# The MLP's operands taken in another order: second half of the tokens projected first, quadrant B21 finished and used last

## The chip, the cores and the metric

The kernel runs on one core of one Trainium2 chip. The metric is the time of one execution on the device, in microseconds (us). The engines of the core work side by side, each through its own list of instructions in order: TensorE (PE) multiplies matrices, VectorE (DVE), ScalarE (ACT) and GpSimd (POOL) work on elements, SyncE (SP) issues most transfers. They meet at semaphores: an instruction waits until the values that it needs have been made, and until the places that it writes have been read by all who still need them.

## The reference, cut to what matters

One layer on 1024 tokens of width 1024: a mixer (forgetting attention beside gated linear attention), a cross-attention on 256 memory tokens, and an MLP of hidden width 4096. Each sub-layer works on the RMS norm of h and adds to h.

```python
h = h + parallel_mixer(rms_norm(h, norm_mix_g), w_in, ..., w_out)
h = h + memory_cross_attention(rms_norm(h, norm_xattn_g), rms_norm(mem, norm_mem_g), ...)   # ends with o @ wo
u = jax.nn.relu(rms_norm(h, norm_mlp_g) @ mlp_w1)
h = h + (u * u) @ mlp_w2
```

All of it is fp32.

## The kernel before, in words

**Products.** fp32 precision is kept with three matmuls for each product: each operand is split into an upper part (a rounded copy, made by ACT) and a lower part (what is left, made by DVE). `gemm` issues, for each 128 rows of the contraction, upper x upper (L107), upper x lower (L108) and lower x upper (L109). `split_into` (L1034) makes a split: ACT's copy is at L1038, DVE's subtraction at L1039. `evac_split` does the same on 512 columns (L114, L115).

**State.** `h`, the transposed activations, lies in SBUF as 8 blocks k of 128 features by 1024 tokens; a *half* is 512 tokens. The MLP is multiplied by the Strassen-Winograd scheme: features and tokens are cut in two, which gives the quadrants b11, b12, b21, b22 of the activations, and seven products replace eight. Its operands are b11, b21, b22 and the combinations t1 = b12 - b11, t2 = b22 - t1, t3 = b22 - b12, t4 = b21 - t2. Each stands in a tile `x` with both parts, 128 x 2048 elements each.

**Order around the change.** `xattn` (the cross-attention) stores its output o through HBM (`od`). `project_o_first` and `project_o_rest` load it (tiles oh, ol; `load_o`) and multiply by wo, in blocks of 24 matmuls (`o_block`), one for each k and half; each adds into h (L841). `finish` (L879 to L883) adds the block's squares to the norm's sum (ACT L165, POOL L166), stores h for the end (`hd`) and scales h in place (DVE L883). Half 0 of the tokens comes before half 1. b11 and b21 are split when half 0 is done; t2 is made block by block beside the last four blocks of half 1 (L909 to L914); t1, t3, b22 and t4 are split at the start of `mlp`.

**The seven stages.** `products7` runs the seven products as stages in the order of `STAGES`. A stage does, for each of two weight blocks (two q), 12 matmuls into a PSUM bank named x, y or w. Every bank is read after each stage (`hidden` in the first product, W1; `output` in the second, W2), also where the next stage adds to the same bank; so that next stage may not start before the bank has been read. In `hidden` the first read of a bank is a copy by ACT (L1131), the later ones are additions by DVE (L1139). They are put into h itself, whose contents are by then split: with `h4`, position c of `c[:, c]` is k 0 (for the first q; 2 for the second) half 0, k 0 half 1, k 1 half 0, k 1 half 1. W1 takes eight rounds p of two q; the results u go to HBM (`ud`), and W2 loads them as its operands into the tiles of the first product's operands, in chunks of 4, 3, 3, 3, 3 q. `weights7` loads a weight block and makes its seven combinations (a11, a12, s1 to s4, a22), each split.

The program is written in this order, but a list scheduler, which knows the cost of each instruction, sets the final order on each engine. The norm's factor of the last step is taken from the squares of the whole h (`token_squares`, `spread`) during W1 and only used at the end.

Of the kernel before, what the change touches and what calls it, by code (L numbers as in the profile page):

```python
# [17 lines left out]
F32 = mybir.dt.float32  # L18
# [12 lines left out]
P = 128  # L31
# [20 lines left out]
class Layer:  # L52
# [774 lines left out]
    def load_o(self, op, half):  # L827

        oh = self.T(op, [P, KT, 512], F32R, "oh")
        ol = self.T(op, [P, KT, 512], F32R, "ol")  # L830
        for k in (slice(k, k + 2) for k in range(0, KT, 2)):
            self.nc.sync.dma_start(f(oh[:, k, :]), self.od[:, 0, half, k, :])
            self.nc.sync.dma_start(f(ol[:, k, :]), self.od[:, 1, half, k, :])
        self.O.append(([oh[:, k, :] for k in range(KT)], [ol[:, k, :] for k in range(KT)]))

    def o_block(self, W, n, half, i, ps, out=None):

# [4 lines left out]

    def project_o_first(self):

        self.ost, self.O = ExitStack(), []
        self.load_o(self.open(self.ost, "op0", side="right"), 0)
        self.Wo = self.wsplit(self.wo[:, 0:512], None)
        for i in range(4):
            self.o_block(self.Wo, 0, 0, i, self.T(self.mmp, [P, 512], F32, "mm"))

    def project_o_rest(self, mx):


        nc = self.nc
        kw = dict(reuse_waits="tile")
        with ExitStack() as st:
            xp = self.open(st, "xp")
# [12 lines left out]
            self.load_o(op1, 1)  # L870
            for i in range(4):
                self.o_block(W, 1, 0, i, next(banks))
            self.ost.close()
            self.acc = [self.T(p, [P, 512], F32, "acc") for p in (xp, self.open(mx, "acc", side="right"))]
            self.X, self.XB = {}, {}
            x0 = self.open(mx, "x0", 3, side="right", **kw)
            h = lambda k, half: self.h[:, k, half * 512:(half + 1) * 512]

            def finish(k, half, src, first):  # L879

                self.add_squares(xp, src, half, first)
                nc.sync.dma_start(self.hd[:, k, half * 512:(half + 1) * 512], src)
                nc.vector.scalar_tensor_tensor(h(k, half), src, self.cols[:, C_MLP + k:C_MLP + k + 1], sB[:, half, :], ALU.mult, ALU.mult)  # L883

            for k in range(KT):
                finish(k, 0, h(k, 0), k == 0)
                if k % 4 == 3:
                    self.operand(("b11", "b21")[k // 4], x0, self.h[:, k - 3:k + 1, 0:512])
            self.token_squares(0, self.yv[:, 0:4])
            for i in range(4):  # L890
                t = self.T(xp, [P, 512], F32, "h2", bufs=2)
                self.o_block(W, 1, 1, i, next(banks), t)
                finish(4 + i, 1, t, i == 0)
            wst.close()
            self.raw7 = self.open(mx, "raw7", 2, side="right", **kw)
            self.ga = self.open(mx, "g7a", 2, side="right", **kw)
# [5 lines left out]
            X = self.X["t2"] = self.T(x0, [P, 2, 4, 512], F32R, "x7")  # L902
            for i in range(4):
                t = self.T(xp, [P, 512], F32, "h2", bufs=2)
                self.o_block(self.Wo, 0, 1, i, next(banks), t)
                finish(i, 1, t, False)
                t2 = self.T(self.s7, [P, 2, 512], F32, "s7")[:, 0, :]
                b11, b21, b12, b22 = h(i, 0), h(4 + i, 0), h(i, 1), h(4 + i, 1)
                nc.vector.tensor_tensor(b11, b12, b11, ALU.subtract)  # L909
                nc.vector.tensor_tensor(t2, b22, b11, ALU.subtract)  # L910
                nc.scalar.activation(X[:, 0, i], t2, AF.Copy)
                nc.vector.tensor_tensor(X[:, 1, i], t2, f(X[:, 0, i]), ALU.subtract)
                nc.vector.tensor_tensor(b12, b22, b12, ALU.subtract)
                nc.vector.tensor_tensor(b21, b21, t2, ALU.subtract)  # L914
            self.XB["t2"] = [X[:, 0, i] for i in range(4)], [X[:, 1, i] for i in range(4)]

    def operand(self, key, pool, src):

# [4 lines left out]
    def xattn(self):  # L923
        nc = self.nc
        with ExitStack() as st:
# [80 lines left out]
            units = [(n, u) for n in range(2) for u in range(4)]  # L1006
            q = []
            for i, (n, u) in enumerate(units):
                if u == 0:
# [18 lines left out]

    STAGES = (("x", "a11", "b11"), ("w", "a12", "b21"), ("x", "s2", "t2"), ("y", "s1", "t1"), ("x", "s3", "t3"),
              ("y", "s4", "b22"), ("x", "a22", "t4"))

    def split_into(self, t, src, n):  # L1034

# [6 lines left out]
    def weights7(self, srcs, n, eng):  # L1042
# [14 lines left out]
        for src, o in zip(srcs, out):  # L1057
            raw = self.T(self.raw7, [P, 4, 512], F32, "raw7")[:, :, 0:n]
            nc.sync.dma_start(raw, src)
            g(o, ("a11", "a12"), raw[:, 0:2])  # L1060
            raws.append(raw)
        yield
        for raw, o in zip(raws, out):
            s = self.T(self.s7, [P, 2, 512], F32, "s7")[:, :, 0:n]
            eng.tensor_tensor(s[:, 0], raw[:, 3], raw[:, 2], ALU.add)  # L1065
            eng.tensor_tensor(s[:, 1], s[:, 0], raw[:, 0], ALU.subtract)
            g(o, ("s1", "s2"), s)
            sa.append(s)
        for raw, o, s2 in zip(raws, out, sa):
            s = self.T(self.s7, [P, 2, 512], F32, "s7")[:, :, 0:n]  # L1070
            eng.tensor_tensor(s[:, 0], raw[:, 0], raw[:, 3], ALU.subtract)
# [1 line left out]
            sb.append(s)  # L1073
        for raw, o, s in zip(raws, out, sb):
            g(o, ("s3", "s4"), s)
            g(o, ("a22",), raw[:, 2:3])
        yield out

    def products7(self, A, B, nk, taken):
# [12 lines left out]
    def mlp(self, mx):  # L1092
        nc = self.nc
        kw = dict(reuse_waits="tile")
        h, X, B = self.h, self.X, self.XB
        x1 = self.open(mx, "x1", 4, **kw)
        self.g4p = self.open(mx, "g74", 2, **kw)
        gb = self.open(mx, "g7b", 2, **kw)
        self.gps, self.ng = [self.ga, self.ga, gb, gb], 2
        my = self.open(mx, "my6", 4, space=PSUM, **kw)  # L1100
# [12 lines left out]
            return next(w)  # L1113

        A = next(self.W1)
        for key, k, half in (("t1", 0, 0), ("t3", 0, 1), ("b22", 4, 1), ("t4", 4, 0)):
            self.operand(key, x1, h[:, k:k + 4, half * 512:(half + 1) * 512])

# [3 lines left out]
        for p in range(NQ // 2):  # L1122
# [3 lines left out]
            def hidden(i, j, ps):  # L1126

                c, t, q = h4[:, i], h4[:, 2 + i], 2 * p + i
                v = c[:, (0, 0, 1, 2, 2, 1, 3)[j]]
                if j in (0, 2, 3):  # L1130
                    nc.scalar.activation(v, ps, AF.Copy)  # L1131
                elif j == 6:
                    nc.scalar.activation(v, ps, AF.Relu)
# [36 lines left out]
        for nk in CHUNKS:  # L1170
# [18 lines left out]
            for o in (0, 2):  # L1189
# [5 lines left out]
                                  nk * P, nc.gpsimd)  # L1195

                def output(i, j, ps):
                    k, half = ((0, 0), (0, 0), (0, 1), (1, 1), (1, 1), (0, 1), (1, 0))[j]
                    k, ts = 2 * (o + i) + k, slice(half * 512, (half + 1) * 512)
                    y = h[:, k, ts]  # L1200
                    if first and j in (0, 2, 3, 6):
# [3 lines left out]
                    if last and j in (1, 4, 5, 6):  # L1205
# [12 lines left out]
def _layout(inputs):  # L1218
# [21 lines left out]
    cols[32:40, C_FB] = a["fox_b_f"]  # L1240
    d["cols"] = cols

    order = [0, 1, 3, 2]
    d["mlp_w1"] = a["mlp_w1"].reshape(2, 4, P, NQ, 2, P).transpose(3, 2, 4, 0, 1, 5).reshape(NQ, P, 4, 512)[:, :, order]
# [21 lines left out]
```

## Time and profile before

| | us |
|---|---|
| three timed runs, median | 1484.55 |
| their lowest and highest | 1483.95, 1484.77 |
| the profiled execution | 1480.27 |
| its span in the profile | 1478.6 |
| PE busy in it | 1430.0 (97%), 7058 matmuls |
| DVE, ACT, POOL busy | 920.8, 681.2, 430.8 |
| mean granted clock of TensorE | 0.988 |

The profile describes one execution. A row of a timeline gives start, duration, engine, line, operation, output tile and inputs, and in brackets how long the engine stood idle before it and what ended that. In a row of windows stand, for a stretch of time, the busy time of each engine with its number of instructions, TensorE's granted clock, the busy share of the DMA engines, and GB/s. A row of waits gives who waited for whom: us in total, how often, and the longest.

The projection of the cross-attention's output lies between about 740 and 847 us of the span, W1 from 847 to about 1177, W2 behind it.

### The profile page before, as it was taken

How to read it: one execution, taken by the hardware profiler on the slowest of the kernel's cores; microseconds unless marked ns; L12 is line 12 of the kernel's file. 1: busy time of each engine (PE TensorE's matmuls, PEld its weight loads, DVE VectorE, ACT ScalarE, POOL GpSimd, SP SyncE). 2: the span in 40 equal slices, each digit the busy share in tenths (PEclk: the TensorE clock that was granted, in tenths of full speed). 3: DMA queues.
4: the chain of work that ended last, by engine and by line, in shares of the span. 5: the costliest groups of instructions: out<-in, count | busy, mean ns of one | idle time of the engine just before them, and what ended most of it. 6: DMA issues, size and time to landing. Idle time of an engine off the chain costs nothing.

```text
span 1478.6 us, 19173 instructions
## 1 busy us (share of the span) xinstructions
PE 1430.0 (97%) x7058; PEld 1195.3 (81%) x7058; DVE 920.8 (62%) x1322; ACT 681.2 (46%) x1092; POOL 430.8 (29%) x457
## 2 busy tenths in 40 slices
PE   7999999999998998999999979999999999999998
PEld 6777788887887787888888868888888888888886
DVE  4396422427776676656654875765565848788686
ACT  4473332326776555445442344544444736335230
POOL 3157503323463412522212300000000342433454
PEclk9999999999999999999999989999999999999999
DMA  8424530259677752413285113544444846337353
GB/s 273 122 54 121 143 86 1 72 173 261 187 203 193 192 158 74 155 40 104 72 279 219 52 63 146 210 171 171 170 169 149 291 159 229 129 109 233 113 201 114
DMA packets 125118, 223.94 MB, mean 151 GB/s; under 512 B 8384, under 2 KB 66528, under 8 KB 118368
## 3 DMA queue, kind: packets, MB, share of 16 engines
q1 hardware_dynamic: 125024, 222.71, 47.0%
q8 instruction: 56, 0.92, 0.2%
q14 instruction: 38, 0.31, 0.1%
HBM read 150.59 MB, written 72.09 MB: 151 GB/s over the span
## 4 chain that ended last, share of the span: by engine, by line
PE 78%; DMA 8%; DVE 7%; ACT 3%; issue 1%; POOL 1%; SPq 0%; POOLq 0%; ACTq 0%; DVEq 0%
PE mm L107 13%; PE mm L108 12%; PE mm L109 12%; PE my L109 7%; PE my L107 7%; PE my L108 7%; PE tr L107 3%; PE tr L108 3%; PE tr L109 3%; DMA raw<-in_w_in_dram 2%; DMA raw<-in_xattn_wkv_dram 2%; PE tr L661 1%; PE pv L668 1%; PE pv L669 1%; PE s L621 1%
## 5 line engine op out<-in xcount | busy, mean ns | idle before, releaser
L109 PE MATMUL my<-x,g 128*128 128x512 f32 x472 | 184.7, 392 | 5.9 <-DVE g L1039 5.8
L107 PE MATMUL my<-x,g 128*128 128x512 f32 x472 | 185.0, 392 | 2.8 <-ACT g L1038 2.8
L108 PE MATMUL my<-x,g 128*128 128x512 f32 x472 | 184.6, 391 | 0.0
L1065 POOL TENSOR_TENSOR s<-raw 128x384 f32<-128x384 f32 (+1 forms) x20 | 25.9, 1297 | 372.0 <-DMA raw<-in_mlp_w_dram 341.4
L1038 ACT ACTIVATE g<-s 128x1024 fp32r<-128x1024 f32 (+1 forms) x72 | 69.0, 963 | 132.8 <-PE my L109 62.3
L108 PE MATMUL mm<-wl,xh 128*128 128x512 f32 x320 | 126.5, 396 | 3.6 <-DVE wl L97 3.6
L107 PE MATMUL mm<-wh,xh 128*128 128x512 f32 x320 | 127.4, 400 | 1.4 <-DVE sq L298 1.4
L109 PE MATMUL mm<-wh,xl 128*128 128x512 f32 x320 | 126.3, 395 | 0.0
L109 PEld LDWEIGHTS my<-x,g 128*128 128x128 f32 x472 | 89.1, 189 | 25.5 <-DVE g L1039 7.0
L107 PEld LDWEIGHTS my<-x,g 128*128 128x128 f32 x472 | 89.2, 189 | 21.8 <-ACT g L1038 3.0
L108 PEld LDWEIGHTS my<-x,g 128*128 128x128 f32 x472 | 89.2, 189 | 18.5
L1039 DVE TENSOR_TENSOR g<-s,g 128x1024 fp32r<-128x1024 f32 (+1 forms) x72 | 85.0, 1186 | 11.1 <-ACT g L1038 10.7
L107 PE MATMUL mm<-x,g 128*128 128x512 f32 x228 | 89.3, 392 | 0.0
L108 PE MATMUL mm<-x,g 128*128 128x512 f32 x228 | 89.2, 391 | 0.0
L109 PE MATMUL mm<-x,g 128*128 128x512 f32 x228 | 88.8, 390 | 0.0
L632 POOL TENSOR_SCALAR p<-p,rrec 128x128 f32<-128x128 f32 (+3 forms) x64 | 50.8, 796 | 128.0 <-DVE rrec L631 115.4
L1039 DVE TENSOR_TENSOR g<-raw,g 128x1024 fp32r<-128x1024 f32 (+3 forms) x72 | 65.4, 910 | 34.2 <-ACT g L1038 34.2
L1178 DVE TENSOR_TENSOR x<-x 128x1024 fp32r<-128x1024 f32 (+1 forms) x64 | 74.4, 1184 | 11.4 <-ACT x L1177 11.1
L97 DVE SCALAR_TENSOR_TENSOR wl<-raw,cols,wh 128x512 fp32r<-128x512 f32 x64 | 49.8, 816 | 48.0 <-ACT wh L96 42.8
L1038 ACT ACTIVATE g<-raw 128x1024 fp32r<-128x1024 f32 (+3 forms) x72 | 55.2, 769 | 48.2 <-PE my L109 20.6
L107 PE MATMUL mm<-wh,sh 128*128 128x512 f32 x192 | 76.3, 399 | 0.7 <-DVE mkv L118 0.4
L108 PE MATMUL tr<-x,g 128*128 128x512 f32 x196 | 76.2, 389 | 0.0
(309 smaller groups left out, 3786.5 us busy)
## 6 DMA issues: line engine op xcount, KB each, us to landing
ud<-h SPq DMA_DIRECT2D x32, 1024.0 KB
x<-ud SPq DMA_DIRECT2D x48, 512.0 KB
raw<-in_mlp_w_dram SPq DMA_DIRECT2D x20, 1024.0 KB
raw<-in_mlp_w_dram SPq DMA_DIRECT2D x16, 768.0 KB
raw<-in_w_in_dram SPq DMA_DIRECT2D x23, 512.0 KB
raw<-in_xattn_wkv_dram SPq DMA_DIRECT2D x16, 512.0 KB
od<-o SPq DMA_DIRECT2D x32, 256.0 KB
xt<-in_x_dram SPq DMA_DIRECT2D x8, 512.0 KB
```

The source lines that it names most:

```text
L97: nc.vector.scalar_tensor_tensor(wl, r, g, f(wh), ALU.mult, ALU.subtract)
L107: mm(ps, lh[k], rh[k], start=start and k == 0, stop=False, **kw)
L108: mm(ps, lh[k], rl[k], start=False, stop=False, **kw)
L109: mm(ps, ll[k], rh[k], start=False, stop=stop and k == n - 1, **kw)
L621: nc.tensor.matmul(ps[:, c], qa[:, ts], ka[:, c], start=True, stop=False)
L632: nc.gpsimd.tensor_scalar(p[:, 0:n], p[:, 0:n], rr, 1.0, ALU.mult, ALU.mult)
L661: nc.tensor.transpose(o, pp[i][:, kb * P:(kb + 1) * P], self.ident)
L668: nc.tensor.matmul(pv, va[:, kb, :], th[:, js], start=kb == 0, stop=False)
L1038: self.nc.scalar.activation(hi, src, AF.Copy)
L1039: self.nc.vector.tensor_tensor(lo, src, f(hi), ALU.subtract)
L1065: eng.tensor_tensor(s[:, 0], raw[:, 3], raw[:, 2], ALU.add)
L1178: nc.vector.tensor_tensor(lo, f(lo), f(hi), ALU.subtract)
```

## The change

The cross-attention's second set of heads takes its token units in the order 2, 3, 0, 1, and the projection does half 1 of the tokens before half 0. The two feature halves are renamed (the rows of W1 are exchanged in the host's layout), so that b11 and b12 are the features of k 4 to 7, and b22 and b21 those of k 0 to 3. b21 is then h of k 0 to 3, half 0, the last four blocks to be projected. b11 and t2 are split during the four blocks before these. The stages are put in the order b11, t1, t2, b22, t3, b21, t4, with the banks x, y, x, y, x, w, x in turns; which reads are copies by ACT changes accordingly. In `mlp`, t1, b22, t3 and b21 are split first; then t2 is put together again from its two parts (L1119), t4 = b21 - t2 is made in place of b21 (L1120) and split. W1's first weight block is loaded and prepared earlier and in another order (a11 first, a12 and a22 last). The squares of half 0 are summed up after p = 1, and the spread comes after p = 3; both came after p = 0.

```diff
     def project_o_first(self):
-        self.load_o(self.open(self.ost, "op0", side="right"), 0)
+        self.load_o(self.open(self.ost, "op0", side="right"), 1)
...
-                self.o_block(self.Wo, 0, 0, i, self.T(self.mmp, [P, 512], F32, "mm"))
+                self.o_block(self.Wo, 0, 1, i, self.T(self.mmp, [P, 512], F32, "mm"))
...
             for k in range(KT):
-                finish(k, 0, h(k, 0), k == 0)
-                if k % 4 == 3:
-                    self.operand(("b11", "b21")[k // 4], x0, self.h[:, k - 3:k + 1, 0:512])
-            self.token_squares(0, self.yv[:, 0:4])
+                finish(k, 1, h(k, 1), k == 0)
+            self.token_squares(1, self.yv[:, 4:8])
...
+                self.o_block(W, 1, 0, i, next(banks), t)
+                finish(4 + i, 0, t, i == 0)
+                t2 = self.T(xp, [P, 512], F32, "t2", bufs=2)
+                b11, b12, b22 = h(4 + i, 0), h(4 + i, 1), h(i, 1)
+                self.evac_split(X1[:, 0, i], X1[:, 1, i], b11)
+                nc.vector.tensor_tensor(b11, b12, b11, ALU.subtract)
+                nc.vector.tensor_tensor(t2, b22, b11, ALU.subtract)
+                self.evac_split(X2[:, 0, i], X2[:, 1, i], t2)
+                nc.vector.tensor_tensor(b12, b22, b12, ALU.subtract)
...
-    STAGES = (("x", "a11", "b11"), ("w", "a12", "b21"), ("x", "s2", "t2"), ("y", "s1", "t1"), ("x", "s3", "t3"),
-              ("y", "s4", "b22"), ("x", "a22", "t4"))
+    STAGES = (("x", "a11", "b11"), ("y", "s1", "t1"), ("x", "s2", "t2"), ("y", "s4", "b22"), ("x", "s3", "t3"),
+              ("w", "a12", "b21"), ("x", "a22", "t4"))
...
-        for key, k, half in (("t1", 0, 0), ("t3", 0, 1), ("b22", 4, 1), ("t4", 4, 0)):
-            self.operand(key, x1, h[:, k:k + 4, half * 512:(half + 1) * 512])
+        half = lambda k, i: h[:, k:k + 4, i * 512:(i + 1) * 512]
+        for key, src in (("t1", half(4, 0)), ("b22", half(0, 1)), ("t3", half(4, 1)), ("b21", half(0, 0))):
+            self.operand(key, x1, src)
+        t2, t4 = half(4, 0), half(0, 0)
+        nc.vector.tensor_tensor(t2, f(X["t2"][:, 0]), f(X["t2"][:, 1]), ALU.add)
+        nc.vector.tensor_tensor(t4, t4, t2, ALU.subtract)
+        self.operand("t4", x1, t4)
...
-                v = c[:, (0, 0, 1, 2, 2, 1, 3)[j]]
-                if j in (0, 2, 3):
+                v = c[:, (0, 2, 1, 1, 2, 0, 3)[j]]
+                if j in (0, 1, 2):
                     nc.scalar.activation(v, ps, AF.Copy)
...
-            if p == 0:
-
-                self.token_squares(1, self.yv[:, 4:8])
+            if p == 1:
+
+                self.token_squares(0, self.yv[:, 0:4])
...
+            if p == 3:
                 F = self.T(self.s7, [P, 2, 512], F32, "s7")
```

The order of ACT at the start of `mlp`, before. The tiles x_1903 to x_1906 are t1, t3, b22 and t4; my_8579 and my_8593 are the banks of stage 0, s and g weights:

```order
619 L1038 ACTIVATE x_1903_8567<-h_5812 128x2048
620 L911 ACTIVATE x_1876_8363<-s_1892_8513 128x512
621 L1038 ACTIVATE x_1904_8570<-h_5812 128x2048
622 L1038 ACTIVATE x_1905_8573<-h_5812 128x2048
623 L1038 ACTIVATE x_1906_8576<-h_5812 128x2048
624 L1131 ACTIVATE h_5812<-my_8579 128x512
625 L1131 ACTIVATE h_5812<-my_8593 128x512
626 L1038 ACTIVATE g_1894_8540<-s_1893_8537 128x1024
```

The same place with the change. x_1902 to x_1906 are t1, b22, t3, b21 and t4; my_8583 and my_8597 are the banks of stages 0 and 2, my_8611 and my_8625 those of stage 1:

```order
621 L1037 ACTIVATE g_1898_8554<-s_1896_8548 128x1024
622 L1037 ACTIVATE g_1899_8557<-s_1897_8551 128x1024
623 L165 ACTIVATE sqT_8529<-h_1893_8502 128x512
624 L1037 ACTIVATE x_1902_8566<-h_5812 128x2048
625 L1037 ACTIVATE x_1903_8569<-h_5812 128x2048
626 L1037 ACTIVATE x_1904_8572<-h_5812 128x2048
627 L1037 ACTIVATE x_1905_8575<-h_5812 128x2048
628 L1037 ACTIVATE x_1906_8580<-h_5812 128x2048
629 L1135 ACTIVATE h_5812<-my_8583 128x512
630 L1135 ACTIVATE h_5812<-my_8597 128x512
631 L1135 ACTIVATE h_5812<-my_8611 128x512
632 L1135 ACTIVATE h_5812<-my_8625 128x512
```

In both orders the first banks are copied behind the copy of t4. With the change that copy of t4 has a new row of DVE before it (L1120), and the banks' copies write into the part of h that t4 is split from. DVE's order there, from the last block of the projection on (mm_8503 is its bank):

```order
775 L841 TENSOR_TENSOR h_1893_8502<-mm_8503,h_5812 128x512
776 L883 SCALAR_TENSOR_TENSOR h_5812<-h_1893_8502,cols_72,sB_7964 128x512
777 L1038 TENSOR_TENSOR g_1898_8554<-s_1896_8548,g_1898_8554 128x1024
778 L1038 TENSOR_TENSOR g_1899_8557<-s_1897_8551,g_1899_8557 128x1024
779 L1038 TENSOR_TENSOR x_1902_8566<-h_5812,x_1902_8566 128x2048
780 L1038 TENSOR_TENSOR x_1903_8569<-h_5812,x_1903_8569 128x2048
781 L1119 TENSOR_TENSOR h_5812<-x_1860_8212 128x4x512
782 L1038 TENSOR_TENSOR x_1904_8572<-h_5812,x_1904_8572 128x2048
783 L1038 TENSOR_TENSOR x_1905_8575<-h_5812,x_1905_8575 128x2048
784 L1120 TENSOR_TENSOR h_5812<-h_5812 128x4x512
785 L1038 TENSOR_TENSOR x_1906_8580<-h_5812,x_1906_8580 128x2048
```

Rows 775 to 784 all stand before t4's split in row 785. The third place is ACT's order at the change from W1 to W2, with the change. mm_10345 is the last bank of W1, x_1905 the tile of b21, into which W2's operands are loaded, L1182 ACT's copy of such an operand:

```order
803 L1138 ACTIVATE h_5812<-h_5812 128x512
804 L1182 ACTIVATE x_1904_8572<-x_1904_8572 128x1024
805 L1037 ACTIVATE g_2076_10611<-s_2074_10605 128x1024
806 L1137 ACTIVATE h_5812<-mm_10345 128x512
807 L1182 ACTIVATE x_1905_8575<-x_1905_8575 128x1024
808 L1146 ACTIVATE h_5812<-h_5812 128x1536
809 L1037 ACTIVATE g_2073_10602<-s_2072_10599 128x1024
810 L1182 ACTIVATE x_1905_8575<-x_1905_8575 128x1024
```

Row 807 waits for a load into a tile that stage 5 of W1's last round still reads; g_2073 is a weight of W2's first round.

More of the change, by code (lines that the diff above doesn't have):

```diff
@@ L833, in load_o @@
             self.nc.sync.dma_start(f(ol[:, k, :]), self.od[:, 1, half, k, :])
-        self.O.append(([oh[:, k, :] for k in range(KT)], [ol[:, k, :] for k in range(KT)]))
+        self.O[half] = [oh[:, k, :] for k in range(KT)], [ol[:, k, :] for k in range(KT)]
     def o_block(self, W, n, half, i, ps, out=None):
@@ L843, in project_o_first @@
     def project_o_first(self):
-        self.ost, self.O = ExitStack(), []
-        self.load_o(self.open(self.ost, "op0", side="right"), 0)
+        self.ost, self.O = ExitStack(), {}
+        self.load_o(self.open(self.ost, "op0", side="right"), 1)
         self.Wo = self.wsplit(self.wo[:, 0:512], None)
         for i in range(4):
-            self.o_block(self.Wo, 0, 0, i, self.T(self.mmp, [P, 512], F32, "mm"))
+            self.o_block(self.Wo, 0, 1, i, self.T(self.mmp, [P, 512], F32, "mm"))
     def project_o_rest(self, mx):
@@ L869, in project_o_rest @@
             self.wps = wps
-            self.load_o(op1, 1)
+            self.load_o(op1, 0)
             for i in range(4):
-                self.o_block(W, 1, 0, i, next(banks))
+                self.o_block(W, 1, 1, i, next(banks))
             self.ost.close()
-            self.acc = [self.T(p, [P, 512], F32, "acc") for p in (xp, self.open(mx, "acc", side="right"))]
-            self.X, self.XB = {}, {}
-            x0 = self.open(mx, "x0", 3, side="right", **kw)
+            self.acc = [self.T(p, [P, 512], F32, "acc") for p in (self.open(mx, "acc", side="right"), xp)]
+            x0 = self.open(mx, "x0", 2, side="right", **kw)
             h = lambda k, half: self.h[:, k, half * 512:(half + 1) * 512]
@@ L885, in project_o_rest @@
             for k in range(KT):
-                finish(k, 0, h(k, 0), k == 0)
-                if k % 4 == 3:
-                    self.operand(("b11", "b21")[k // 4], x0, self.h[:, k - 3:k + 1, 0:512])
-            self.token_squares(0, self.yv[:, 0:4])
+                finish(k, 1, h(k, 1), k == 0)
+            self.token_squares(1, self.yv[:, 4:8])
+            X1, X2 = (self.T(x0, [P, 2, 4, 512], F32R, "x7") for _ in range(2))
+            self.X = {"b11": X1, "t2": X2}
+            self.XB = {n: tuple([X[:, j, i] for i in range(4)] for j in range(2)) for n, X in self.X.items()}
             for i in range(4):
                 t = self.T(xp, [P, 512], F32, "h2", bufs=2)
-                self.o_block(W, 1, 1, i, next(banks), t)
-                finish(4 + i, 1, t, i == 0)
+                self.o_block(W, 1, 0, i, next(banks), t)
[7 more added lines that the diff above has]
+                nc.vector.tensor_tensor(b12, b22, b12, ALU.subtract)
             wst.close()
             self.raw7 = self.open(mx, "raw7", 2, side="right", **kw)
+            self.g4p = self.open(mx, "g74", 2, side="right", **kw)
             self.ga = self.open(mx, "g7a", 2, side="right", **kw)
@@ L900, in project_o_rest @@
             next(self.W1)
-            X = self.X["t2"] = self.T(x0, [P, 2, 4, 512], F32R, "x7")
             for i in range(4):
                 t = self.T(xp, [P, 512], F32, "h2", bufs=2)
[L905 to L915, printed above, removed]
+                self.o_block(self.Wo, 0, 0, i, next(banks), t)
+                finish(i, 0, t, False)
     def operand(self, key, pool, src):
@@ L1004, in attend @@
                                                   u % 2 * 256:u % 2 * 256 + 256], f(o[:, i]))
-            units = [(n, u) for n in range(2) for u in range(4)]
+            units = [(0, u) for u in range(4)] + [(1, u) for u in (2, 3, 0, 1)]
             q = []
             for i, (n, u) in enumerate(units):
-                if u == 0:
+                if i % 4 == 0:
                     weights(n)
@@ L1059, in weights7 @@
             nc.sync.dma_start(raw, src)
-            g(o, ("a11", "a12"), raw[:, 0:2])
+            g(o, ("a11",), raw[:, 0:1])
             raws.append(raw)
-        yield
         for raw, o in zip(raws, out):
@@ L1068, in weights7 @@
             sa.append(s)
+        yield
         for raw, o, s2 in zip(raws, out, sa):
@@ L1075, in weights7 @@
             g(o, ("s3", "s4"), s)
-            g(o, ("a22",), raw[:, 2:3])
+        for raw, o in zip(raws, out):
+            g(o, ("a12", "a22"), raw[:, 1:3])
         yield out
@@ L1095, in mlp @@
         h, X, B = self.h, self.X, self.XB
-        x1 = self.open(mx, "x1", 4, **kw)
-        self.g4p = self.open(mx, "g74", 2, **kw)
+        x1 = self.open(mx, "x1", 5, **kw)
         gb = self.open(mx, "g7b", 2, **kw)
@@ L1197, in output @@
                 def output(i, j, ps):
-                    k, half = ((0, 0), (0, 0), (0, 1), (1, 1), (1, 1), (0, 1), (1, 0))[j]
+                    k, half = ((0, 0), (1, 1), (0, 1), (0, 1), (1, 1), (0, 0), (1, 0))[j]
                     k, ts = 2 * (o + i) + k, slice(half * 512, (half + 1) * 512)
                     y = h[:, k, ts]
-                    if first and j in (0, 2, 3, 6):
+                    if first and j in (0, 1, 2, 6):
                         nc.scalar.activation(y, ps, AF.Copy)
@@ L1204, in output @@
                         nc.vector.tensor_tensor(y, ps, y, ALU.add)
-                    if last and j in (1, 4, 5, 6):
+                    if last and j in (3, 4, 5, 6):
                         nc.vector.tensor_tensor(y, y, F[:, half], ALU.mult)
@@ L1241, in _layout @@
     d["cols"] = cols
-    order = [0, 1, 3, 2]
-    d["mlp_w1"] = a["mlp_w1"].reshape(2, 4, P, NQ, 2, P).transpose(3, 2, 4, 0, 1, 5).reshape(NQ, P, 4, 512)[:, :, order]
+    order, swapped = [0, 1, 3, 2], [1, 0, 2, 3]
+    d["mlp_w1"] = a["mlp_w1"].reshape(2, 4, P, NQ, 2, P).transpose(3, 2, 4, 0, 1, 5).reshape(NQ, P, 4, 512)[:, :, swapped]
     d["mlp_w2"] = a["mlp_w2"].reshape(NQ, 2, P, 4, 2, P).transpose(3, 2, 4, 1, 0, 5).reshape(4, P, 4, NQ, P)[:, :, order]
```

## The prediction

> **What bounds the kernel now.** I read the page first, then 10 us windows over the join of the cross-attention's projection and the MLP, then PE's waits, and last the timelines of PE, ACT and DVE through that join.
>
> ```profile
> span 1478.6 us, 19173 instructions
> PE 1430.0 (97%) x7058; PEld 1195.3 (81%) x7058; DVE 920.8 (62%) x1322; ACT 681.2 (46%) x1092; POOL 430.8 (29%) x457
> ```
>
> TensorE is the bound. The change keeps its instructions, so only PE's idle or slowly clocked time can move. From 735 us on, the part that the change touches, PE waits three times:
>
> ```profile
> PE my L109 <- DVE g L1039: 5.8, 1, 5.8
> PE my L107 <- ACT g L1038: 2.8, 1, 2.8
> PE mm L107 <- DMA oh<-od: 0.7, 1, 0.7
> ```
>
> The first two lie together (window, PE busy and count, PEld, DVE, ACT, POOL, then PE's granted clock):
>
> ```profile
> 840.00:850.00 10.00, 10.00 (x46) 8.26 (x44) 9.86 (x15) 3.69 (x6) 1.31 (x2) 1.00 0.08 29
> 850.00:860.00 10.00, 8.76 (x41) 7.07 (x39) 9.97 (x13) 8.33 (x7) 2.79 (x1) 1.00 0.07 26
> 860.00:870.00 10.00, 3.27 (x8) 2.06 (x8) 10.00 (x9) 3.47 (x5) 0.19 (x1) 0.61 0.29 106
> 870.00:880.00 10.00, 9.45 (x31) 7.62 (x32) 6.39 (x11) 3.20 (x4) 0.00 (x0) 0.71 0.29 105
> ```
>
> While PE starves, DVE is full: it is DVE that is late, with the splits of the MLP's operands. PE through the join:
>
> ```profile
> 847.05 0.39 PE L109 MATMUL mm<-oh,wl 128*128 128x512 f32 x1
> 847.28 0.39 PE L107 MATMUL my<-x,g 128*128 128x512 f32 x1
> 847.50 0.39 PE L108 MATMUL my<-x,g 128*128 128x512 f32 x1
> ...
> 858.16 0.60 PE L173 MATMUL tr<-ident,acc 128*128 128x128 f32 x4
> 861.51 0.50 PE L107 MATMUL my<-x,g 128*128 128x512 f32 x1 [2.76 <-ACT g L1038]
> ...
> 862.87 0.63 PE L107 MATMUL my<-x,g 128*128 128x512 f32 x1
> ...
> 870.55 0.80 PE L109 MATMUL my<-x,g 128*128 128x512 f32 x1 [5.78 <-DVE g L1039]
> 871.15 0.63 PE L107 MATMUL my<-x,g 128*128 128x512 f32 x1
> ...
> 875.41 0.57 PE L107 MATMUL mm<-x,g 128*128 128x512 f32 x1
> 875.82 0.39 PE L108 MATMUL mm<-x,g 128*128 128x512 f32 x1
> ```
>
> A matmul takes 0.227 us from start to start at full clock (847.28 to 847.50) and 0.43 us at the granted clock of about 0.5 (12 matmuls from 870.55 to 875.82 take 5.27). Between 847.28 and 875.82, 28.5 us, PE does stages 0 and 1 (48 matmuls), four transposes (0.6) and 20 more matmuls. 68 x 0.227 + 0.6 = 16.0, so this join loses **12.5 us**, the most that the change can win there: 0.84% of the span.
>
> **The change, part by part.**
>
> *Projection in the other order.* The 192 matmuls of each half only change places. The split of b11 and t2 (512 columns at a time, L114 and L115) now lies beside the o-blocks of half 0, where a block lasts 24 x 0.227 = 5.4 us of PE against two ACT copies and seven DVE rows of about 0.7 each; PE covers both. If not covered, the excess would be under 1 us in all. W1's first loads leave SP's queue ahead of the projection's oh/ol loads, and the loads of half 0 now stand behind all stores of o. PE's one wait there is the 0.7 above: between -0.7 and +1.5 (two more such waits), taken as 0.
>
> *The join itself.* This carries the sum. These are the rows of before that price it:
>
> ```profile
> 848.48 0.69 DVE L841 TENSOR_TENSOR h<-mm,h 128x512 f32<-128x512 f32 x1
> 849.68 0.75 DVE L883 SCALAR_TENSOR_TENSOR h<-h,cols,sB 128x512 f32<-128x512 f32 x1
> 851.67 1.68 DVE L910 TENSOR_TENSOR s<-h 128x512 f32<-128x512 f32 x1
> 855.68 2.28 DVE L1039 TENSOR_TENSOR x<-h,x 128x2048 fp32r<-128x2048 f32 x1
> 859.68 4.48 DVE L1039 TENSOR_TENSOR x<-h,x 128x2048 fp32r<-128x2048 f32 x2
> 869.29 3.48 DVE L1039 TENSOR_TENSOR g<-s,g 128x1024 fp32r<-128x1024 f32 x3
> 849.26 0.63 ACT L165 ACTIVATE sqT<-h 128x512 f32<-128x512 f32 x1 [0.63 <-DVE h L841]
> 854.03 5.52 ACT L1038 ACTIVATE x<-h 128x2048 fp32r<-128x2048 f32 x3
> 859.46 1.06 ACT L1131 ACTIVATE h<-my 128x512 f32<-128x512 f32 x2
> 860.41 2.00 ACT L1038 ACTIVATE g<-s 128x1024 fp32r<-128x1024 f32 x2
> ```
>
> After the last o-block DVE has to do: L841 (0.6 start to start), L883 (0.7), two 128x1024 splits of s1/s2 (1.16 each), then six 128x2048 rows at 2.24: the lower parts of t1, b22, t3, b21, and the two tensor subtractions or additions that make t2 again and t4 (L1119, L1120). No trace shows these two; the nearest row is the 128x2048 split, same engine and size. Last comes the lower part of t4.
>
> ACT runs ahead of it: from 847.5, two g copies (2.0), the square (0.6), t1's upper part (1.84), done at 851.95. DVE takes t1's lower part then, and its six rows end at 851.95 + 6 x 2.24 = 865.4. Only then can ACT make t4's upper part (1.9, 867.3) and DVE its lower part (2.28, 869.6).
>
> What PE waits for is not t4's product, which is the last of the seven. It is the **first bank's eviction**. Stage 0's result is copied into h at k 0 (and 2), half 0. There b21 lay, and t4 is made in place of it, so the copy must overwrite nothing that t4's split has yet to read. ACT's order says so: the four copies at L1135 stand behind t4's copy, and the first waits for the DVE row after it. Before, the same copy went over t1's old place, whose split on DVE ended at 855.68 + 2.28. Stage 2 adds into the bank of stage 0, so it cannot start before that copy: 869.6 + 0.6 = 870.2.
>
> PE meanwhile: stage 0 ends at 847.28 + 24 x 0.227 = 852.7; two matmuls of stage 1, then a wait of about 1.0 for t1's lower part; stage 1 ends at 859.2. It idles for 11 us, and should restart at the slow clock like the row at 870.55 does, for as long (12 matmuls). One price more: DVE's 512-wide rows can be held while POOL adds squares (L910 above: 1.68 against the usual 0.69). One such row now lies on the chain: 0 to 1.1, taken as 0.5, so 870.7.
>
> The Trainium skill ("SBUF — State Buffer", section on who interferes with whom) says that a DVE instruction with two SBUF inputs contends with a GpSimd instruction that reads SBUF; the row at 851.67 agrees. The same skill ("TensorE: Matmul & The Clock Gate", Part 1) has the clock fall after an idle window of about 3.4 us and rise after 3.4 us of busy; here a matmul already took 0.63 at 862.87, behind an idle time of 2.76, and the clock rose only after 5.3, so the trace is taken. By the page, the restart would be some 0.9 cheaper (an estimate from its 3.4 us).
>
> Before, PE came back for good at 870.55 with 48 matmuls, four transposes and 8 more matmuls done. After, it comes back at 870.7 with 48 done. So the join costs 0.15 + 8 x 0.227 + 0.6 = **+2.6 us** (1.5 to 3.8).
>
> *The rms of half 0 and its spread, after p = 1 and p = 3.* The transposes are counted above. The spread's L183 rows now stand in DVE's order among a running pair's evictions; before they lay in the hole. From 0 (no PE wait there before) to one 128x1024 row ahead of them, 1.16: **+0.4**.
>
> *b21's tile is free later.* In W2 the operand tiles hold the next products: the first group (b11, b21) of four q sits in the tiles of b11 and b21. Before, b21's tile was free after stage 1, five stages of 5.4 us ahead of W2; now after stage 5, one stage ahead, while ACT, DVE and DMA are busy (same columns as above, DMA's share and GB/s last):
>
> ```profile
> 1140.00:1150.00 10.00, 10.00 (x46) 8.29 (x45) 4.85 (x5) 4.79 (x7) 3.31 (x2) 1.00 1.02 407
> 1150.00:1160.00 10.00, 10.00 (x46) 8.29 (x45) 7.64 (x8) 8.55 (x10) 2.72 (x3) 1.00 0.93 343
> 1160.00:1170.00 10.00, 10.00 (x46) 8.29 (x45) 10.00 (x10) 10.00 (x11) 4.39 (x2) 1.00 0.67 216
> ...
> 1171.42 1.47 ACT L1142 ACTIVATE h<-h 128x1536 f32<-128x1536 f32 x1
> ...
> L1177 ACT ACTIVATE x<-x 128x1024 fp32r<-128x1024 f32 x48 | 50.3, 1056 | 22.2 <-DMA x<-ud 22.1
> ```
>
> Queued on ACT behind the copy that waits for b21's load stand a square (1.47) and W2's s1 copy (about 1.06, with 1.25 of DVE after it), which PE needs 24 matmuls into W2, the products on other tiles being put ahead. So the copy (1.06) must start by 5.4 - 4.8 = 0.6 after W1's last matmul, 6.0 after stage 5 frees the tile. A load of 512 KB takes 1.4 us at the 375 GB/s of the first two windows; with four loads and a 1 MB block of W2 ahead of it in the queues, 1.4 + 5.6 + 2.8 = 9.8. So it comes between in time and 3.8 late: half, **+1.9**. The four later changes of chunk have the same short lead with three q: 0 to 2, **+0.3** together.
>
> *Sum:* 2.6 + 0.4 + 1.9 + 0.3 = +5.2 us. The profiled execution took 1480.27 us, 1.67 outside its span; 1485.5 after. The three timed runs have a median 4.28 above it: 1484.55 + 5.2 = **1489.8 us**. With every term at its lower end (1.5 and -0.7): 1485.4; at its upper end (1.5 + 3.8 + 1.2 + 3.8 + 2.0 = 12.3): 1496.9.
>
> **The rivals.**
>
> *The hole closes (faster).* b21 is finished last and used last; if nothing holds stage 2, PE waits only for t1's lower part (1.0) and whatever t4 is late by at stage 6, which starts no sooner than 847.3 + 6 x 5.4 = 880: nothing. Gain up to 12.5 - 1.0 = 11.5: 1473. For it: DVE's work after the last o-block is spread better. Against it: ACT's order, where the copy of the first bank stands behind t4.
>
> *No change that can be told.* The same hole with its terms at their lower ends (the restart shorter, the spread and the load of b21 hidden): +1.5, 1486. A measurement of this kernel can tell about 0.2%, 3 us, from no change. For it: before, no join of MLP stages after 880 us makes PE wait at all.
>
> *The late tile decides (slower by more).* If the load of b21 stands behind others in the queues at every change of product set, a whole stage is lost at W2's start (5.4) and 1 at each later chunk (4.0): 2.6 + 0.4 + 5.4 + 4.0 = +12.4, 1497. It decides once the load takes over 6 us. For it: the DMA share of 0.93 to 1.02 above. Against it: before, PE waits nowhere in W2, with three q a chunk.
>
> **How the numbers follow.** Forecast 0.55 (its own range 1486.5 to 1494), no change 0.22, hole closes 0.12, late tile 0.11. Of the forecast, 0.05 lies within 0.2%. So slower 0.50 + 0.11 = 0.61, same 0.22 + 0.05 = 0.27, faster 0.12. The range reaches from 1481 to 1497, leaving out the closed hole and the worse half of the late tile.
>
> **What would show it.** In the profile after: PE idle of 10 to 12 us in one piece from about 859, ended by ACT's copy at L1135; a wait of about 1 before it, on DVE's L1038; the clock about 0.5 for 5 us; t4's DVE row before the copy. PE waits at W2's start, released by ACT or DVE at the group b11/b21. The forecast is wrong if PE goes on from stage 1 to stage 2 without a wait on L1135, or if the hole is of a size with these rows but PE waits elsewhere for over 3 us.

## The result

The changed kernel takes **1517.74 us** (median of four runs, 1515.54 to 1518.83), against 1484.66 for the kernel before (four runs): a ratio of 1.0222, 95% interval 1.0204 to 1.0240. It is 33 us slower. The prediction said slower, by 5 us, with a range up to 1497.

The page after, its first lines:

```profile
span 1517.0 us, 19134 instructions
PE 1438.9 (95%) x7058; PEld 1196.6 (79%) x7058; DVE 936.4 (62%) x1323; ACT 682.6 (45%) x1095; POOL 435.2 (29%) x457
```

The matmuls are as many as before, and PE is busy for 95% of the span in place of 97%. The join first. PE after (start, duration, engine, line, output and inputs, idle time ahead and what ended it):

```profile
851.63 0.39 PE L107 MATMUL my<-x,g 128*128 128x512 f32 x1
...
858.99 0.50 PE L108 MATMUL my<-x,g 128*128 128x512 f32 x1 [1.31 <-DVE x L1038]
...
875.08 0.80 PE L107 MATMUL my<-x,g 128*128 128x512 f32 x1 [10.81 <-ACT h L1135]
```

ACT and DVE there:

```profile
870.10 1.91 ACT L1037 ACTIVATE x<-h 128x2048 fp32r<-128x2048 f32 x1 [8.76 <-DVE h L1120]
874.43 2.06 ACT L1135 ACTIVATE h<-my 128x512 f32<-128x512 f32 x4 [2.42 <-DVE x L1038]
853.28 3.45 DVE L1038 TENSOR_TENSOR g<-s,g 128x1024 fp32r<-128x1024 f32 x2
867.78 2.29 DVE L1120 TENSOR_TENSOR h<-h 128x2048 f32<-128x2048 f32 x1
872.05 2.29 DVE L1038 TENSOR_TENSOR x<-h,x 128x2048 fp32r<-128x2048 f32 x1 [1.98 <-ACT x L1037]
```

PE does stages 0 and 1 and then waits 10.8 us for ACT's copy of the first bank, which stands behind t4's copy (870.10) and t4's lower part (872.05 to 874.34). L1120, which no trace of before had shown, took 2.29.

That is not where the 33 us are. The waits of PE from 1178 us on, the end of W1 and W2, where the kernel before had none above 0.2 us:

```profile
PE mm L107 <- DVE h L1209: 6.1, 3, 3.1
PE mm L109 <- DVE g L1038: 4.5, 1, 4.5
PE my L107 <- ACT g L1037: 3.7, 2, 2.8
PE tr L108 <- DVE x L1183: 2.4, 2, 1.9
PE tr L107 <- DVE h L1209: 1.6, 1, 1.6
PE mm L107 <- ACT g L1037: 1.5, 1, 1.5
PE my L109 <- DVE g L1038: 1.1, 1, 1.1
```

They sum to 21 us, and windows of 40 us show where they lie (PE busy and count, PEld, DVE, ACT, POOL, granted clock, DMA's share, GB/s):

```profile
1160.00:1200.00 40.00, 33.73 (x139) 26.82 (x138) 32.52 (x29) 25.53 (x31) 14.87 (x8) 0.91 0.65 244
...
1360.00:1400.00 40.00, 36.09 (x148) 27.91 (x147) 30.58 (x35) 16.56 (x20) 10.83 (x8) 0.96 0.52 178
1440.00:1480.00 40.00, 36.65 (x161) 29.71 (x160) 33.72 (x38) 11.61 (x15) 19.42 (x14) 1.00 0.49 183
```

A full window holds about 178 matmuls. One window lies at the change from W1 to W2, the others at changes of W2's chunks. By the count of matmuls W1 ends, and W2 starts, at 1167 us in the kernel before (not at about 1177) and at 1174 in the changed one.

For all that follows the MLP is measured by itself, from the start of its first matmul to the start of its last. Before it took 624.9 us (847.28 to 1472.21), after 658.2 (851.63 to 1509.86): **+33.3**. The rest of the two spans' difference of 38.4 is 3.9 us by which the second execution was behind already at the cross-attention's first product on the memory keys, ahead of what the change moves in time (the profiled execution of before was 4 us under its median), 0.5 at the projection and 0.7 behind the last matmul.

### The profile page after: what moved, and what is told of

Same layout as the page of the kernel before. It is cut to its first block, busy times and chain, and to the rows that moved or that the text cites. A ratio compares the mean times of both kernels' runs of the same rounds, so it can differ in the third digit from the quotient of the medians.

```text
span 1517.0 us, 19134 instructions
## 1 busy us (share of the span) xinstructions
PE 1438.9 (95%) x7058; PEld 1196.6 (79%) x7058; DVE 936.4 (62%) x1323; ACT 682.6 (45%) x1095; POOL 435.2 (29%) x457
## 4 chain that ended last, share of the span: by engine, by line
PE 72%; DMA 10%; DVE 9%; ACT 3%; issue 3%; POOL 2%; SPq 0%; POOLq 0%; DVEq 0%; ACTq 0%
PE mm L107 12%; PE mm L108 12%; PE mm L109 12%; PE my L107 5%; PE my L108 5%; PE my L109 5%; PE tr L108 3%; PE tr L109 3%; PE tr L107 3%; DMA raw<-in_w_in_dram 2%; DMA x<-ud 2%; DMA raw<-in_xattn_wkv_dram 2%; DVE g L1038 1%; DMA raw<-in_mlp_w_dram 1%; DVE x L1183 1%
## 5 line engine op out<-in xcount | busy, mean ns | idle before, releaser
L107 PE MATMUL my<-x,g 128*128 128x512 f32 x472 | 186.2, 396 | 14.7 <-ACT h L1135 10.8
L1038 DVE TENSOR_TENSOR g<-raw,g 128x512 fp32r<-128x512 f32 (+3 forms) x72 | 75.3, 1047 | 114.5 <-ACT g L1037 114.3
L1037 ACT ACTIVATE g<-raw 128x512 fp32r<-128x512 f32 (+3 forms) x72 | 55.7, 774 | 167.9 <-DMA raw<-in_mlp_w_dram 59.4
L1038 DVE TENSOR_TENSOR g<-s,g 128x1024 fp32r<-128x1024 f32 (+1 forms) x72 | 90.4, 1257 | 34.1 <-ACT g L1037 34.1
L107 PE MATMUL mm<-x,g 128*128 128x512 f32 x220 | 87.4, 397 | 7.6 <-DVE h L1209 6.1
L109 PE MATMUL mm<-x,g 128*128 128x512 f32 x220 | 87.0, 396 | 4.5 <-DVE g L1038 4.5
L108 PE MATMUL mm<-x,g 128*128 128x512 f32 x220 | 86.6, 394 | 0.0
L108 PE MATMUL tr<-x,g 128*128 128x512 f32 x204 | 80.3, 393 | 2.4 <-DVE x L1183 2.4
L107 PE MATMUL tr<-x,g 128*128 128x512 f32 x204 | 79.3, 391 | 1.6 <-DVE h L1209 1.6
L109 PE MATMUL tr<-x,g 128*128 128x512 f32 x204 | 80.0, 392 | 0.0
```

The costliest lines, as they stand in the source:

```text
L107: mm(ps, lh[k], rh[k], start=start and k == 0, stop=False, **kw)
L108: mm(ps, lh[k], rl[k], start=False, stop=False, **kw)
L109: mm(ps, ll[k], rh[k], start=False, stop=stop and k == n - 1, **kw)
L1037: self.nc.scalar.activation(hi, src, AF.Copy)
L1038: self.nc.vector.tensor_tensor(lo, src, f(hi), ALU.subtract)
```

## The experiments

Each is an edit of the changed kernel. Times are single executions unless an interval is given; the MLP's length and PE's waits are from the profile. An edit shifts the line numbers behind it, so the same line of code can be L1135 in one kernel and L1143 in another.

### W2 in the old order

W2 goes back to the stage order and the weight preparation of before.

```diff
-            self.products7(A, B, nk, output)
+            self.products7(A, B, nk, output, self.STAGES2)   # STAGES2: the order of before
 ...
+            g(o, ("a11", "a12"), raw[:, 0:2]) ... g(o, ("a22",), raw[:, 2:3])   # in W2: weights7 as before
```

> Only W2 goes back to the stage order and the weight preparation of before; W1, the projection and the tiles stay as changed. Against the changed kernel (1517.7 us, 21 us of PE's waits from 1180 us on). Theory A (b21's tile comes free one stage before the next product set needs it): the waits at the four later changes of chunk go, since b21 is then used at stage 1 again, but the one at W2's start stays (6.3 us of waits and some 2 of slow clock), because W1 still frees the tile after its stage 5: about 1517.7 - 20 = 1498. Theory B (W2's weights come late, since both raw blocks are freed only behind the splits of a12 and a22, and s1 is needed at stage 1 in place of stage 3): all of W2's waits go, W2's start too: about 1489. Rival C (the loss has nothing to do with W2's order): no change, 1517.

1493.3 us; MLP 632.5, **25.7 less** than changed. PE's waits from 1150 us on:

```profile
PE tr L109 <- DVE g L1040: 3.1, 2, 2.7
PE my L109 <- DVE g L1040: 1.1, 1, 1.1
PE my L107 <- ACT h L1215: 0.6, 1, 0.6
```

All lie at W2's start; the waits at the later changes of chunk are gone. Rival C falls. The time lies between the two theories (1498 and 1489). The pattern is that of theory A, but what is left at W2's start is nearly all waits on weights (g), which is B's word.

### Other tiles for W2's operands

W2 keeps the new order and the new weight preparation. Only the tiles that W2's operands are loaded into change, so that b21 does not share a tile with b11, and with them the order of the loads: b11's come first.

```diff
-        groups = ((("b11", "b21"), slots(X["b11"], X["b21"]), slice(0, 4, 3)),
-                  (("t1", "t2"), ...), (("b22", "t3"), ...), (("t4",), slots(X["t4"]), slice(7, 8)))
+        groups = ((("t1", "t2"), ...), (("b22", "t3"), ...),
+                  (("b21", "t4"), slots(X["b21"], X["t4"]), slice(3, 8, 4)),
+                  (("b11",), slots(X["b11"]), slice(0, 1)))
 ...
-            for names, room, which in groups:
+            for names, room, which in groups[3:] + groups[:3]:
```

> W2 keeps the new order and the new weight preparation; only the tiles that the operands of W2 are loaded into change: b11 has a tile of its own, b21 shares two tiles with t4, so every tile comes free at least five stages before it is needed. Theory A: PE's waits of W2 go nearly all, about 1517.7 - 28 = 1490. Theory B: the waits on operands (x and h, 10 us) shrink, those on weights (g, 11 us) stay with their slow clock: 1503 to 1508.

1495.6 us; MLP 638.1, **20.1 less**. PE's waits from 1150 us on:

```profile
PE mm L109 <- DVE g L1038: 4.2, 1, 4.2
PE mm L107 <- DVE h L1209: 1.6, 2, 1.0
PE my L107 <- DVE h L1209: 1.4, 3, 1.1
```

The time lies between theory A (1490) and theory B (1503 to 1508). Behind W2's start 3 us of waits are left, and none of them on g, though a chunk's raw weight blocks are loaded as late as in the changed kernel (for the third chunk 15.9 us ahead of it, 15.8 there). So at the later chunks most of the loss comes with the late tile, the waits on weights too. How a late tile stops weights and banks is seen in the loads and in DVE's order. The loads of the third chunk's operands, before and after, as SP issues them (the chunk starts, by the count of matmuls, at 1301.1 and at 1318.6):

```profile
1279.28 22.08 SPq L1176 DMA_DIRECT2D x<-ud  x12
```

```profile
1300.92 1.72 SPq L1181 DMA_DIRECT2D x<-ud  x3
...
1309.08 9.84 SPq L1181 DMA_DIRECT2D x<-ud  x9
```

These are three loads for each of the four groups. By the count of matmuls each group is loaded as its places in the tiles come free. Before, the group (b11, b21) leaves first, 21.8 us ahead of the chunk; after, third, 5.4 ahead. The other groups are no later: (t1, t2) leaves 17.7 us ahead where it was 13.7, (b22, t3) 9.5 where it was 5.5, t4 1.4 as before. So the late tile holds back its own three loads alone, but nine loads in place of six now fall into the last 10 us. At the chunk's start DVE has five of its nine splits of 128x1024 still to begin, where it had two, and DVE, which has no idle gap from 1316 to 1330, does them between the evictions:

```profile
1320.45 1.75 DVE L1038 TENSOR_TENSOR g<-s,g 128x768 fp32r<-128x768 f32 x1
1322.12 0.68 DVE L1209 TENSOR_TENSOR h<-mm,h 128x512 f32<-128x512 f32 x1
```

The eviction at 1322.12 ends PE's wait of 2.70 at 1322.86. PE waits for a bank whose last matmul had ended by 1316.8, because splits stand ahead of its eviction in DVE's order.

### Only W1's first round in the new order

The other seven rounds of W1, and W2, have the order and the weight preparation of before. The join is untouched.

```diff
-            self.products7(A, B, 4, hidden)
+            self.products7(A, B, 4, hidden, self.STAGES2 if p else self.STAGES)
 ...
+            # p >= 1: weights7 and the choice of copies as before
```

> The changed kernel, with the new stage order and weight preparation in the first round of W1 only; the join is untouched. If all that the change costs behind the first round comes from the order of stages and weights in the later rounds and in W2, this leaves the join's +2.6 us over before and nothing else: about 1487. If the spread after p = 3 or the earlier W1 loads cost something, it is more.

1487.0 us; MLP 627.7, **+2.8** over before. PE's waits from 735 us on:

```profile
PE my L107 <- ACT h L1143: 10.8, 1, 10.8
PE my L108 <- DVE x L1040: 1.3, 1, 1.3
PE mm L107 <- DMA oh<-od: 1.1, 1, 1.1
PE my L184 <- DVE dg L183: 0.2, 1, 0.2
```

The join is as in the changed kernel, and the MLP has no other wait but 0.2 for the moved spread. So the join costs 2.8 with the spread in it, and all the rest comes from the order in which the later rounds and W2 use stages and prepare weights.

### What holds the first bank's copy

t4 is made in t2's place, in the same order.

```diff
-        nc.vector.tensor_tensor(t4, t4, t2, ALU.subtract)
-        self.operand("t4", x1, t4)
+        nc.vector.tensor_tensor(t2, t4, t2, ALU.subtract)
+        self.operand("t4", x1, t2)
```

> t4 is made in the place of t2 instead of in the place of b21, in the same order. The copy of the first bank then has only to wait until t2 has been subtracted (L1120, which ended at 870.07 in the changed kernel) and not for t4's lower part (874.34). By my account, ACT makes t4's upper part first, being in order, and the copy comes 1.9 us after L1120: PE's wait shrinks from 10.8 to 8.4. If the copy waited for something other than t4's split, the wait stays at 10.8.

The wait shrinks to 8.15 us (8.4 expected). ACT and DVE in this run:

```profile
874.84 1.91 ACT L1037 ACTIVATE x<-h 128x2048 fp32r<-128x2048 f32 x1 [8.64 <-DVE h L1120]
876.66 2.04 ACT L1135 ACTIVATE h<-my 128x512 f32<-128x512 f32 x4
876.78 2.29 DVE L1038 TENSOR_TENSOR x<-h,x 128x2048 fp32r<-128x2048 f32 x1 [1.98 <-ACT x L1037]
```

The copy no longer waits for t4's lower part, which starts after it, only for its turn behind t4's upper part. The whole took 1516.5 us, MLP 651.1; the 7 us are more than this wait, since W2's waits, untouched here, also came out smaller. Of such single runs only the wait itself is used.

Then t2 and t4 are made earlier in the program:

```diff
+        self.operand("t1", x1, t2)
+        nc.vector.tensor_tensor(t2, f(X["t2"][:, 0]), f(X["t2"][:, 1]), ALU.add)
+        nc.vector.tensor_tensor(t2, t4, t2, ALU.subtract)
+        for key, src in (("b21", t4), ("b22", half(0, 1)), ("t3", half(4, 1)), ("t4", t2)):
+            self.operand(key, x1, src)
```

> As the run before, and t2 and t4 are made right behind t1's split, ahead of the splits of b21, b22 and t3. DVE then does t1's lower part, L1119, the subtraction and b21's lower part before the copy is free: 856.7 + 4 x 2.24 = 865.6, copy done by 866.3. PE's wait of 10.8 shrinks to about 2.5, and the time by 8 to 10 us (1508 to 1510), with the waits of W2 unchanged. If the wait came from DVE's load as such, whatever its order, it would stay near 10.8.

The wait was 8.16, not 2.5 (1518.9 us, MLP 655.3). The edit did not reach the engine:

```profile
864.20 2.28 DVE L1118 TENSOR_TENSOR h<-x 128x2048 f32<-128x2048 f32 x1
866.40 4.48 DVE L1038 TENSOR_TENSOR x<-h,x 128x2048 fp32r<-128x2048 f32 x2
870.80 2.28 DVE L1119 TENSOR_TENSOR h<-h 128x2048 f32<-128x2048 f32 x1
```

Two splits still stand between t2 and t4. The scheduler, not the place in the program, sets DVE's order, so for the join this run repeats the one before it and says nothing on earlier work.

### The join streamed

t1 is split beside the projection too, t2 made in t1's place and t4 in t2's, block by block; the weights' g tiles are opened later; W2 is in the old order; and W2's first operands go to the tiles that W1 frees first.

```diff
+                self.evac_split(X3[:, 0, i], X3[:, 1, i], b11)              # t1, beside the o-blocks
+                nc.vector.tensor_tensor(b11, b22, b11, ALU.subtract)         # t2 in t1's place
+                self.evac_split(X2[:, 0, i], X2[:, 1, i], b11)
 ...
                 finish(i, 0, t, False)
+                nc.vector.tensor_tensor(h(4 + i, 0), h(i, 0), h(4 + i, 0), ALU.subtract)   # t4 in t2's place
 ...
+        groups = ((("b11", "b21"), slots(X["b11"], X["t1"]), ...), (("t1", "t2"), slots(X["t2"], X["b22"]), ...),
+                  (("b22", "t3"), slots(X["t3"], X["b21"]), ...), ...)
```

> W2 as in the run with W2's old order, W1 in the new order. Two more edits. (1) The join: t1, too, is split block by block beside the projection, t2 is made in t1's place, and t4 in t2's place as each block of b21 arrives, so that nothing but the splits of b21, b22, t3 and t4 is left for DVE after the last block; the weights' g tiles are opened later to make room. My account: the first bank's copy is then held only by ACT's own rows, PE's wait of 10.8 becomes under 2.5, and the slow clock behind it goes: 12 us less at the join. (2) At W2's start the tiles that take W2's operands are those that W1 frees first (b11 and t1, then t2 and b22, then t3 and b21). If b21's late tile causes the 4.9 us of waits on g at W2's start that W2's old order left, they go; if W1's last raw weight blocks, freed late, cause them, they stay. Time: 1493.3 - 12 = 1481 with the waits at W2's start, 1475 without.

1484.4 us (ten runs), ratio to before 0.9992 (0.9978 to 1.0007): no difference. MLP 624.6. The join's wait is 2.69; at W2's start 5.2 us of waits stay (1.01 on g at 1179, 4.14 on an eviction at 1186). The early tile did not help there. What the eviction waited for is a store of W1's results out of the place in h that it writes:

```profile
1175.88 0.55 SPq L1059 DMA_DIRECT2D raw<-in_mlp_w_dram  x1
1176.52 0.57 SPq L1146 DMA_DIRECT2D ud<-h  x1
1185.42 0.60 ACT L1214 ACTIVATE h<-my 128x512 f32<-128x512 f32 x1 [7.54 <-DMA ud<-h]
```

ACT had made the values by 1171.42. The store left only at 1176.52, because SP issues in order and the load of a weight block of W2's second pair stood ahead of it, waiting for its raw place, which POOL's sums of the first pair had read until 1175.86.

The same with only the first round of W1 in the new order:

```diff
+            self.products7(A, B, 4, hidden, self.STAGES2 if p else self.STAGES)
```

> As the run before, but only the first round of W1 has the new stage order and weight preparation; the other seven rounds and W2 have those of before, with the tiles of before. Both candidates for W2's start (late tile, late raw blocks) are then gone: no wait there. The join as in the run before. Expected 1484.7 - 12 = 1473, if the change of order between the first and the second round costs nothing.

**1478.2 us** (five runs, 1477.6 to 1479.2), ratio to before **0.9955** (0.9941 to 0.9969): 7 us faster than before and 40 faster than changed. MLP 617.2, 7.7 less than before. PE's waits from 735 us on:

```profile
PE my L107 <- ACT h L1142: 2.7, 1, 2.7
...
PE my L107 <- ACT h L1214: 0.5, 1, 0.5
```

The gain is 5 us under my 12; 2.7 us of wait and a restart at the slow clock are left at the join:

```profile
864.66 1.04 ACT L1038 ACTIVATE g<-s 128x1024 fp32r<-128x1024 f32 x1
865.60 2.04 ACT L1142 ACTIVATE h<-my 128x512 f32<-128x512 f32 x4
866.23 0.80 PE L107 MATMUL my<-x,g 128*128 128x512 f32 x1 [2.69 <-ACT h L1142]
```

The copy needs nothing now but its turn: four splits and a weight stand ahead of it on ACT.

### W2's start: late tile or late raw blocks

In the kernel just shown, the tile of W2's first group is made as late as it was in the changed kernel, at W2's start alone; the raw weight blocks stay early.

```diff
-        groups = ((("b11", "b21"), slots(X["b11"], X["b21"]), slice(0, 4, 3)),
+        groups = ((("b11", "b21"), slots(X["b11"], X["b22"]), slice(0, 4, 3)),
 ...
-                  (("b22", "t3"), slots(X["t3"], X["b22"]), slice(2, 6, 3)),
+                  (("b22", "t3"), slots(X["t3"], X["b21"]), slice(2, 6, 3)),
```

> The kernel of the run with only W1's first round in the new order and the join streamed (its MLP took 617.2 us, with 0.5 us of waits at W2's start), where W1's raw weight blocks come free early. One edit: W2's first group (b11, b21) is loaded into the tiles of b11 and b22 in place of b11 and b21, and the group (b22, t3) into those of t3 and b21. In the last round of W1 b22's tile comes free after stage 5, so at W2's start, and only there, this tile is as late as b21's was in the changed kernel, with raw blocks early. If the late tile causes the 4 to 6 us of waits at W2's start, they come back: MLP 622 to 624. If the late raw blocks cause them, there are none: 617 to 618.

1479.9 us, MLP 617.5: no loss, and the same single wait of 0.5 us from 1150 us on. So a late tile alone costs nothing at W2's start. There it holds two of four q, so that PE can begin with the other two; at the later chunks all three loads of the group come late. Whether that is the difference was not tried. The four kernels with W1's new weight preparation (changed, W2 in the old order, other tiles, the first streamed one) wait there 4 to 6 us, whether the tile is early or late; the three with it in the first round only wait at most 0.5. W2's first weight block, as SP issues it, before and after:

```profile
1129.41 0.57 SPq L1059 DMA_DIRECT2D raw<-in_mlp_w_dram  x1
```

```profile
1151.82 0.57 SPq L1058 DMA_DIRECT2D raw<-in_mlp_w_dram  x1
```

W1's last round starts at 1129.34 in the one and at 1135.67 in the other, by the count of matmuls: the block is loaded as the round starts before, and 16 us into it with the change. The new order of preparation holds for every weight block of W1 and W2, not for the first alone. It splits a12 and a22 last, and their g tile is that of s1 and s2, free only after stage 2, which ends about then; until then the raw block is held, and the next load into its place. POOL then makes eight sums for the pair, of 1.3 to 2.3 us each, between 1160.9 and 1180.8 (before, 1136.5 to 1165.3), and their splits fall where ACT and DVE have no time left (each busy for 10.0 of the 10 us from 1170). In the first streamed kernel the rows above show the way from the late block to PE. That the raw block's release is the part that counts was not tried by itself: the four kernels also differ from the three in the order of stages and of splits in W1's later rounds.

## Why the prediction was wrong

**The join was right, in mechanism and size.** Forecast: a wait of about 1.0 on t1, then one of 11 until ACT's copy of the first bank, held by t4's split; cost +2.6. Measured: 1.31, 10.81 and +2.8. The contention that I priced at 0.5 was there: two splits of s1 and s2 took 3.45 where two of before's three take 2.32. Of these 1.1 us, 0.4 reached the end of the chain: t4's lower part ended 22.7 us behind the MLP's first matmul, 22.3 by my sum without the contention. The run with t4 elsewhere moved the wait as the account says.

**The spread** was put at +0.4 and is 0.2; **the projection's loads** were put at 0 and cost 0.5 (oh's wait is 1.4 against 0.7).

**W2's start had the wrong cause and too small a size.** The step said that b21's tile comes late there and priced a load 1.9 late. Measured: 4.8 us, the MLP of W2 in the old order against that of the kernel with only the first round new, and the late tile contributes nothing that shows. In the changed kernel itself PE's one wait there on an operand is 0.2. What comes late is the raw weight block, and with it the sums; the rows of the first streamed kernel show it as the cause for 4.1 us, elsewhere it is the likeliest reading. The prediction has no term for it: it took the new order of preparation as a matter of W1's first block and did not ask when a raw block becomes free. The row to ask was SP's issue of that block, at 1129.41 in before.

**The later changes of chunk are the step that failed.** It said: "the same short lead with three q: 0 to 2, +0.3 together". Measured: W2's new order costs 25.7, of which other tiles alone give back 20.1. The mechanism, a tile that comes free one stage before it is needed, was named, and also as a rival, which had the right direction; but its price, 1 us for each later chunk in the rival, was not worked out from any row. I put against that rival that PE waits nowhere in W2 before; but before, the loads had five stages of lead, so that was no evidence for one stage. And I priced a load and its split, not DVE's list: three more splits come behind the chunk's start, ahead of evictions that PE waits for. Four such changes cost about 5 us each, with the slow clock.

The sum of the three steps in us of the MLP: join 2.8 (627.7 - 624.9), W2's start 4.8 (632.5 - 627.7), W2's order 25.7 (658.2 - 632.5). They add up to the whole by the way they are taken; three kernels with the same W2 (changed, and the two with t4 elsewhere) took 336.1, 332.1 and 335.9 us for it, so the last two steps are not known closer than some 4 us. What is left of the 25.7 when the tiles are put right, 5.6, is open: it may be that s1 is needed at stage 1 in place of stage 3, or the raw blocks.

The rival that the hole closes was rightly given little. The hole shrank, from 10.8 to 2.7, only when t1's split and the making of t4 moved beside the projection, block by block, and t4 lay elsewhere.

## What to carry to other kernels

When the order of use of operands changes in a loop that reloads their tiles, write down for each tile after which stage it comes free and before which the next pass needs it: a lead that falls from five stages to one needs a price, and a trace without waits at the old lead does not excuse it. Price it by the in-order lists in which the late item stands: what the engine that splits it also evicts, and what else the issuing queue holds behind a load that waits. Do the same for the raw block that a new order of splits holds longer. And an operand that is made late must not lie where early results are written.

## What the runs showed of the hardware

The granted clock's fall did not follow the length of a gap alone. In the changed kernel a gap of 2.70 us at 1322.86 was followed by a full start and then by slow matmuls (0.63 in place of 0.39), one of 3.06 at 1451.46 by none:

```profile
1322.86 0.50 PE L107 MATMUL mm<-x,g 128*128 128x512 f32 x1 [2.70 <-DVE h L1209]
...
1324.35 0.63 PE L109 MATMUL mm<-x,g 128*128 128x512 f32 x1
...
1451.46 0.47 PE L107 MATMUL mm<-x,g 128*128 128x512 f32 x1 [3.06 <-DVE h L1209]
...
1452.00 0.40 PE L109 MATMUL mm<-x,g 128*128 128x512 f32 x1
```

The Trainium skill ("TensorE: Matmul & The Clock Gate", Part 1) says that the clock is set by a free-running window of about 3.4 us, so that where in the window a gap falls matters. These two rows agree with that; that even a gap under 3.4 us can bring the slow clock, as at 1322.86, is not what its table says.

The traces show the grid itself. In the ten traces the granted clock is 1.00 or 0.50. Every slow stretch, but for the last of a trace, lasts 3.41 us or a whole multiple of it (13.65 at the join of the changed kernel), and all those of one run start whole steps of 3.41 apart. Windows cut along the steps of this run (us, PE's busy time and count, PEld, DVE, ACT, POOL, granted clock, DMA's share, GB/s):

```profile
1320.42:1323.84 3.42, 0.98 (x4) 0.85 (x5) 3.42 (x4) 3.28 (x4) 2.65 (x2) 1.00 0.50 184
1323.84:1327.25 3.41, 3.41 (x9) 2.65 (x9) 3.41 (x5) 3.41 (x6) 0.00 (x0) 0.50 0.00 0
...
1446.72:1450.13 3.41, 1.68 (x8) 1.04 (x6) 3.41 (x3) 0.63 (x2) 3.18 (x2) 1.00 1.01 404
1450.13:1453.55 3.42, 2.09 (x9) 1.77 (x10) 3.42 (x5) 3.42 (x5) 0.00 (x0) 1.00 0.43 168
```

The gap of 2.70 us falls nearly whole into one step, which has 0.98 us of PE's work, and the next step is slow. The longer gap is divided between two steps, which keep 1.68 and 2.09 us of work, and none is slow. Where the limit lies between these is not shown.
